# First-layer modulation products in steps of 256 columns instead of 512

## The chip, the cores and the metric

The kernel runs on one core of one Trainium2 chip. The metric is the device time of one execution in microseconds (us), the median of several runs. A second number is used beside it: one execution was taken by the hardware profiler, and all views of the trace come from that one.

## The reference

Two layers of a trunk for a diffusion model. Each layer has a mixer and an MLP, and around both of them an adaptive norm (shift, scale, gate). The six modulation vectors of a layer come from one product, of a vector per condition with a weight of 1024 x 6144:

```python
def _modulation(cond, w, b):
    m = jax.nn.silu(cond) @ w + b
    return jnp.split(m[:, None, :], 6, axis=-1)
...
    p_sh1, p_sc1, p_g1, p_sh2, p_sc2, p_g2 = _modulation(c_ctx[None, :], ada_w[l], ada_b[l])
    s_sh1, s_sc1, s_g1, s_sh2, s_sc2, s_g2 = _modulation(c, ada_w[l], ada_b[l])
    hp = _rmsnorm(xp, norm_g[l, 0]) * (1.0 + p_sc1) + p_sh1
    hs = _rmsnorm(xs, norm_g[l, 0]) * (1.0 + s_sc1) + s_sh1
    ...
    xp = xp + p_g1 * mp
    xs = xs + s_g1 * ms
    hp = _rmsnorm(xp, norm_g[l, 1]) * (1.0 + p_sc2) + p_sh2
    hs = _rmsnorm(xs, norm_g[l, 1]) * (1.0 + s_sc2) + s_sh2
    xp = xp + p_g2 * _mlp(hp, w_mlp1[l], w_mlp2[l])
    xs = xs + s_g2 * _mlp(hs, w_mlp1[l], w_mlp2[l])
```

There are 128 context tokens (`xp`) and 256 latent ones (`xs`), of width 1024, all in float32. The mixer of layer 0 is a pair of recurrences, HGRN2 and a gated delta rule; the delta rule solves triangular systems of 32 x 32. The mixer of layer 1 is neighbourhood attention.

## The kernel before, in words

Tokens are held as three tiles of 128, the width 1024 as eight k-tiles of 128 (`KT`). Weights are loaded as float32, split into a high part (`whi`, L209) and a low part (`wlo`, L210), and each product is three matmuls: high by high, low by high, high by low (rows L646 to L648 and L688 to L690 of the profile, 384 or 256 columns each).

Layer 0 (`layer0`) writes its work in an order set by hand, the string `STEPS` (L55 to 58). Each word is a piece: `f`, `q`, `c`, `v`, `g` are blocks of projections of the tokens, `h` a step of the HGRN2 recurrence, `d` a step of the delta rule, `a` a step of the modulation products, and a number behind `h`, `d` or `a` is a count of such steps. The framework's scheduler then places the instructions of each engine by its own simulation, so the order on an engine isn't the order of the string word for word.

The modulation products of layer 0 come in three parts. The shift and scale for the mixer are made in front of all else (L446, in passes of 256 columns). The change is in the other two, which `ada_rest` (L373) makes while the mixer runs:

- `ada_quad` (L314): the columns 2048 to 4095 (gate of the mixer and shift of the MLP), as 4 groups of 512 columns. It takes 8 steps, one for each k-tile. A step loads two tiles of 512 KB (L324) and runs 4 matmuls (L327); each has a stationary of 32 columns (the conditions) and a moving operand of 512 columns, and writes 32 of the 128 rows of one accumulator (`ada`). Four such matmuls use four column groups of the PE array.
- `ada_half` (L354): the columns 4096 to 5119 (scale of the MLP) as 2 groups of 512 columns, with the 8 k-tiles as two halves in parallel: 4 steps, each again with two tiles of 512 KB (L363) and 4 matmuls (L368).

The tiles come from a ring of two (`adr=2` in the pool `spa`). A step takes both, so its loads wait until the matmuls of the step before are done with them. Behind `ada_quad` the gate goes to memory (`gs`, L389) and the shift is spread over partitions (L489).

SP issues all loads and stores of the kernel in one order, and a load that waits for its ring holds back what stands behind it: the weight loads (`raw`, L204), the ring's loads (`adr`), and the way in and out of the triangular solve: `g` to memory and back (`s`, `sm`: L1057, L1058, L1062), the solve on GpSimd (L1071, L1072 in turn, 31 times), its result to memory (`s<-sm`, L1074) and back (`hyB<-s`, L1076). TensorE's L1105 and DVE's L1078 wait for hyB. The convolution of the delta rule has a pair of operations on GpSimd (L947, L948) between the solve's; TensorE's transpose (L953) waits for it.

## Time and profile before

| what | value |
|---|---|
| median of 3 runs | 1148.52 us (1146.92 to 1149.19) |
| the profiled execution, its own time | 1152.35 us |
| its span in the trace | 1150.6 us |
| mean granted TensorE clock | 0.976 |
| TensorE busy | 1088.7 us (95%), 6861 instructions |
| DVE, ACT, POOL busy | 760.7, 490.1, 289.9 us |
| L327 matmuls | 71.6 to 175.8 us |
| L368 matmuls | 198.9 to 281.3 us |

Times in rows are microseconds from the start of the span. A row of the chain of waits has a start, a length and what ran; a row of the timeline has the same with the engine, line, tiles and shapes, and in brackets the idle time ahead of it with what ended it. `SPq` is the queue of SP, which issues transfers. One float32 matmul of the program shows as two records, so four matmuls are "x8".

### The profile page before, as it was taken

To read this page: it belongs to the slowest core of one execution; us is meant where nothing else is said; L and a number is where in the kernel's file an instruction comes from. 1 tells how busy PE (TensorE), PEld (TensorE's weight loads), DVE (VectorE), ACT (ScalarE), POOL (GpSimd) and SP (SyncE) were. 2 spreads that over 40 slices of the span, in tenths; PEclk is the share of its full clock that TensorE was granted. 3 is DMA by queue.
4 is the path that set the end of the run, shared out by engine and by line. 5 is a ranking of instruction groups with operands and counts; after the bars stand their busy time and mean duration, and the time that the engine had idled before them with its cause. 6 is when DMAs were issued, how large, how long until landed. Compare 5 with 4: busy or idle time off the path is not lost.

```text
span 1150.6 us, 18007 instructions
## 1 busy us (share of the span) xinstructions
PE 1088.7 (95%) x6861; PEld 943.6 (82%) x6861; DVE 760.7 (66%) x1186; ACT 490.1 (43%) x874; POOL 289.9 (25%) x301
## 2 busy tenths in 40 slices
PE   6989978999899899999999989999988999999998
PEld 3868767988888888898889878888768889989987
DVE  3678598895356697986898565877757763333333
ACT  3465333333354553333343455555635433433330
POOL 0064894231222210120121334424012011101102
PEclk9989988999799899999999999999999999999999
DMA  8953624333043597775774228666524964333311
GB/s 283 292 166 112 215 97 131 114 109 126 19 129 110 176 318 274 255 245 178 238 242 161 74 55 196 192 181 158 142 74 126 331 192 138 128 114 125 110 37 56
DMA packets 142091, 184.66 MB, mean 160 GB/s; under 512 B 36803, under 2 KB 113685, under 8 KB 142005
## 3 DMA queue, kind: packets, MB, share of 16 engines
q1 hardware_dynamic: 141685, 183.44, 50.6%
q8 instruction: 54, 0.88, 0.3%
q14 instruction: 32, 0.26, 0.1%
q10 hardware_dynamic: 320, 0.07, 0.0%
HBM read 171.53 MB, written 4.61 MB: 153 GB/s over the span
## 4 chain that ended last, share of the span: by engine, by line
PE 73%; DMA 7%; POOL 7%; DVE 6%; SPq 3%; issue 2%; ACT 2%; POOLq 0%; DVEq 0%; ACTq 0%
PE acc L1344 7%; PE tmp L1359 7%; PE tmp L1360 7%; PE acc L1346 7%; PE acc L1345 7%; PE tmp L1358 7%; POOL sm L1071 2%; POOL sm L1072 2%; DMA ada<-in_ada_w 2%; PE acc L646 2%; PE acc L647 2%; PE po L1735 2%; PE acc L673 2%; PE acc L674 1%; PE acc L648 1%
## 5 line engine op out<-in xcount | busy, mean ns | idle before, releaser
L209 ACT ACTIVATE whi<-raw 128x1024 fp32r<-128x1024 f32 x198 | 205.9, 1050 | 331.3 <-PE acc L1346 212.0
L210 DVE TENSOR_TENSOR wlo<-raw,whi 128x1024 fp32r<-128x1024 f32 x192 | 237.3, 1246 | 162.7 <-ACT whi L209 159.4
L1378 POOL TENSOR_TENSOR h<-h 128x384 f32<-128x384 f32 x56 | 69.9, 1248 | 423.7 <-ACT h L1375 408.2
L1345 PE MATMUL acc<-wlo,h 128*128 128x512 f32 x380 | 148.5, 391 | 0.0
L1344 PE MATMUL acc<-whi,h 128*128 128x512 f32 x380 | 146.2, 393 | 0.1
L347 DVE SCALAR_TENSOR_TENSOR adc<-adr,scz,adc 128x1024 f32<-128x1024 f32 x98 | 127.8, 1335 | 9.4 <-DMA adr<-in_ada_w 9.2
L1346 PE MATMUL acc<-whi,h 128*128 128x512 f32 x380 | 121.1, 391 | 0.0
L1344 PEld LDWEIGHTS acc<-whi,h 128*128 128x128 f32 x380 | 71.1, 188 | 20.1 <-ACT whi L209 5.6
L1359 PE MATMUL tmp<-hyA,whi 128*128 128x384 f32 (+1 forms) x256 | 85.2, 333 | 2.1 <-DVE hyA L566 2.1
L1358 PE MATMUL tmp<-hyA,whi 128*128 128x384 f32 (+1 forms) x256 | 84.3, 335 | 1.5 <-ACT whi L209 1.5
L1360 PE MATMUL tmp<-hyA,wlo 128*128 128x384 f32 (+1 forms) x256 | 84.9, 333 | 0.0
L1358 PE MATMUL tmp<-hyB,whi 128*128 128x384 f32 (+1 forms) x256 | 83.7, 329 | 1.2 <-DVE hyB L565 1.2
L1359 PE MATMUL tmp<-hyB,whi 128*128 128x384 f32 (+1 forms) x256 | 84.1, 329 | 0.7 <-DVE hyB L566 0.7
L1345 PEld LDWEIGHTS acc<-wlo,h 128*128 128x128 f32 x380 | 71.4, 188 | 14.0 <-DVE wlo L210 0.2
L1346 PEld LDWEIGHTS acc<-whi,h 128*128 128x128 f32 x380 | 71.0, 188 | 13.7
L1360 PE MATMUL tmp<-hyB,wlo 128*128 128x384 f32 (+1 forms) x256 | 82.1, 328 | 0.0
L646 PE MATMUL acc<-hyA,whi 128*128 128x384 f32 x208 | 74.7, 359 | 0.9 <-DVE hyB L707 0.9
L647 PE MATMUL acc<-hyA,whi 128*128 128x384 f32 x208 | 72.3, 348 | 0.0
L648 PE MATMUL acc<-hyA,wlo 128*128 128x384 f32 x208 | 72.0, 347 | 0.0
L1379 DVE TENSOR_TENSOR h<-h,h 128x384 fp32r<-128x384 f32 (+2 forms) x72 | 38.5, 535 | 41.1 <-POOL h L1378 40.5
L526 POOL TENSOR_TENSOR ss<-ss,eps 128x1 f32<-128x1 f32 (+2 forms) x30 | 35.7, 1194 | 68.9 <-DVE ss L545 21.1
L1359 PEld LDWEIGHTS tmp<-hyA,whi 128*128 128x128 f32 x256 | 49.3, 193 | 3.3 <-DVE hyA L566 2.3
(458 smaller groups left out, 2402.9 us busy)
## 6 DMA issues: line engine op xcount, KB each, us to landing
raw<-in_w_mlp SPq DMA_DIRECT2D x128, 512.0 KB, 3.8
adr<-in_ada_w SPq DMA_DIRECT2D x80, 512.0 KB, 4.7
raw<-in_w_in_ab SPq DMA_DIRECT2D x34, 512.0 KB, 4.5
ada<-in_ada_w SPq DMA_DIRECT2D x32, 256.0 KB, 5.5
raw<-in_w_qkv_na SPq DMA_DIRECT2D x32, 256.0 KB, 3.1
raw<-in_w_out_ab SPq DMA_DIRECT2D x8, 512.0 KB, 4.0
m<-gs SPq DMA_DIRECT2D x8, 512.0 KB
raw<-in_w_qkv_na SPq DMA_DIRECT2D x8, 512.0 KB
```

Source lines behind the costliest of these rows:

```text
L209: self.nc.scalar.activation(hi, x, AF.Copy)
L210: (eng or self.nc.vector).tensor_tensor(lo, x, hi.bitcast(F32), op=ALU.subtract)
L347: nc.vector.scalar_tensor_tensor(acc[v], raw, s[v], acc[v], op0=ALU.mult, op1=ALU.add)
L646: nc.tensor.matmul(pg[n], whi(k)[:, c], hhi[:, k], start=(k == 0), stop=False)
L647: nc.tensor.matmul(pg[n], whi(k)[:, c], hlo[:, k], start=False, stop=False)
L648: nc.tensor.matmul(pg[n], wlo(k)[:, c], hhi[:, k], start=False, stop=(k == KT - 1))
L1344: nc.tensor.matmul(pg, shi, w2hi(n)[:, o], start=start, stop=False)
L1345: nc.tensor.matmul(pg, shi, w2lo(n)[:, o], start=False, stop=False)
L1346: nc.tensor.matmul(pg, slo, w2hi(n)[:, o], start=False, stop=last)
L1358: nc.tensor.matmul(pg[n], w1hi(k)[:, c], hhi[:, k, tc_], start=(k == 0), stop=False)
L1359: nc.tensor.matmul(pg[n], w1hi(k)[:, c], hlo[:, k, tc_], start=False, stop=False)
L1360: nc.tensor.matmul(pg[n], w1lo(k)[:, c], hhi[:, k, tc_], start=False, stop=(k == KT - 1))
```

## The change

The modulation products go in half steps. The outer loop is now over the two halves of 256 columns of each group of 512, and the inner over the k-tiles. A half step takes one tile of the ring, 512 KB, and runs its 4 matmuls on 256 columns. In `ada_quad` one transfer fills a tile, with runs of 1 KB where it had 4 KB before; in `ada_half` there are two transfers of 256 KB for each tile. `ada_rest` has 24 steps where it had 12, and the counts behind `a` in `STEPS` are doubled in the same places. The ring stays at two tiles, and all bytes are the same.

```diff
-d f3 f1 f2 d q1 a2 q0 d h a2 h a h c4 h a d h3 d c5 h a2 d h v0 h d h d v1 a d h3
-c0 h3 c1 h5 d2 h d2 h d h7 g0 g1 d m g2 g3 a3
+d f3 f1 f2 d q1 a4 q0 d h a4 h a2 h c4 h a2 d h3 d c5 h a4 d h v0 h d h d v1 a2 d h3
+c0 h3 c1 h5 d2 h d2 h d h7 g0 g1 d m g2 g3 a6
...
-        for kt in range(KT):
-            w = []
-            for j in range(0, 4, 2):
-                raw = self.sb([P, 2, 512], self.ada_ring)
-                rows = i["ada_w"][l, kt * P:(kt + 1) * P]
-                nc.sync.dma_start(raw, rows[:, cols[j]:cols[j] + D].rearrange("p (j n) -> p j n", j=2))
-                w += [raw[:, n] for n in range(2)]
-            for j in range(4):
-                nc.tensor.matmul(pm[32 * j:32 * j + 32], self.sc[:, 2 * kt:2 * kt + 32], w[j], start=(kt == 0), stop=(kt == KT - 1))
-            if kt < KT - 1:
-                yield
+        for c in range(2):
+            for kt in range(KT):
+                w = self.sb([P, 4, 256], self.ada_ring)
+                rows = i["ada_w"][l, kt * P:(kt + 1) * P, col:col + 4 * 512]
+                nc.sync.dma_start(w, rows.rearrange("p (j c n) -> p j c n", j=4, c=2)[:, :, c])
+                for j in range(4):
+                    nc.tensor.matmul(pm[32 * j:32 * j + 32, 256 * c:256 * c + 256], self.sc[:, 2 * kt:2 * kt + 32], w[:, j],
+                                     start=(kt == 0), stop=(kt == KT - 1))
+                if c == 0 or kt < KT - 1:
+                    yield
...
-        for r in range(4):
-            w = []
-            for g in range(2):
-                w.append(self.sb([P, 2, 512], self.ada_ring))
-                nc.sync.dma_start(w[g], i["ada_w"][l, (4 * g + r) * P:(4 * g + r + 1) * P, col:col + D].rearrange("p (n c) -> p n c", n=2))
-            for g in range(2):
-                kt = 4 * g + r
-                for n in range(2):
-                    j = 2 * g + n
-                    nc.tensor.matmul(pm[32 * j:32 * j + 32], self.sc[:, 2 * kt:2 * kt + 32], w[g][:, n], start=(r == 0), stop=(r == 3))
-            if r < 3:
-                yield
+        for c in range(2):
+            for r in range(4):
+                w = self.sb([P, 2, 2, 256], self.ada_ring)
+                for g in range(2):
+                    rows = i["ada_w"][l, (4 * g + r) * P:(4 * g + r + 1) * P, col:col + D]
+                    nc.sync.dma_start(w[:, g], rows.rearrange("p (n c m) -> p n c m", n=2, c=2)[:, :, c])
+                for g in range(2):
+                    kt = 4 * g + r
+                    for n in range(2):
+                        j = 2 * g + n
+                        nc.tensor.matmul(pm[32 * j:32 * j + 32, 256 * c:256 * c + 256], self.sc[:, 2 * kt:2 * kt + 32], w[:, g, n],
+                                         start=(r == 0), stop=(r == 3))
+                if c == 0 or r < 3:
+                    yield
```

In the new file every line from `ada_rest` on has a number higher by 2 (L1105 is L1107, L688 is L690); L327 becomes L326, L363 and L368 become L364 and L369.

The scheduler moves instructions around these steps. Three places matter to the prediction. The first is on PE, where it comes to the first matmul on the solve's result (`gd<-hyB`); `acc` are product rows, `hyA` the normed tokens. Before:

```order
L688 MATMUL acc_2209<-whi_2201,hyA_128 128x256
L689 MATMUL acc_2209<-whi_2201,hyA_129 128x256
L690 MATMUL acc_2209<-wlo_2202,hyA_128 128x256
L1105 MATMUL gd_927<-hyB_649,m_120_753 32x32 [waits DMAHW4_49]
L1105 MATMUL gd_927<-hyB_649,m_120_753 32x32 x11
L1105 MATMUL gd_940<-hyB_649,m_120_753 32x32 x12
L953 MATMUL tmp_1876<-ident,cv_1873 128x128 [waits Pool_49] x2
L953 MATMUL tmp_1876<-ident,cv_1873 128x128
L688 MATMUL acc_2209<-whi_2205,hyA_130 128x256
```

Now:

```order
L690 MATMUL acc_2241<-whi_2237,hyA_130 128x256
L691 MATMUL acc_2241<-whi_2237,hyA_131 128x256
L692 MATMUL acc_2241<-wlo_2238,hyA_130 128x256
L1107 MATMUL gd_927<-hyB_649,m_120_753 32x32 [waits DMAHW3_49]
L1107 MATMUL gd_927<-hyB_649,m_120_753 32x32 x11
L1107 MATMUL gd_940<-hyB_649,m_120_753 32x32 x12
L690 MATMUL acc_2241<-whi_2233,hyA_128 128x256
L691 MATMUL acc_2241<-whi_2233,hyA_129 128x256
L692 MATMUL acc_2241<-wlo_2234,hyA_128 128x256
```

Before, 36 rows of this `acc` stand ahead of the wait for hyB and 12 behind it; now 24 stand ahead and 24 behind. The transpose L953 (now L955) moves further back.

The second place is on SP, around the store of the solve's result (`s<-sm`) and its way back (`hyB<-s`). Before:

```order
L204 DMA raw_2542<-in_w_in_ab 128x4x256 [waits DMAHW6_49,DVE_49]
L363 DMA adr_2287<-in_ada_w 128x1024 [waits DMAHW1_49,PE_49]
L1074 DMA s_842<-sm_139_850 24x32x32 [waits Pool_49]
L1074 DMA s_842<-sm_139_850 24x32x32
L1074 DMA s_842<-sm_139_850 24x32x32 [waits DMAHW7_49]
L1074 DMA s_842<-sm_139_850 24x32x32 [waits DMAHW0_49]
L363 DMA adr_2289<-in_ada_w 128x1024 [waits DMAHW2_49,PE_49]
L389 DMA gs_1940<-ada_1260 2x512 [waits DVE_49]
L389 DMA gs_1940<-ada_1260 2x512 [waits DMAHW3_49]
L1076 DMA hyB_649<-s_842 128x768 [waits DMAHW6_49,DMAHW5_49,DMAHW7_49,DMAHW4_49,DMAHW0_49]
```

Now:

```order
L204 DMA raw_2580<-in_w_in_ab 128x4x256 [waits DMAHW6_49,DVE_49]
L1076 DMA s_842<-sm_139_850 24x32x32 [waits Pool_49]
L1076 DMA s_842<-sm_139_850 24x32x32 x2
L1076 DMA s_842<-sm_139_850 24x32x32 [waits DMAHW7_49]
L364 DMA adr_2319<-in_ada_w 128x2x256 [waits DMAHW1_49,DMAHW0_49,PE_49]
L364 DMA adr_2319<-in_ada_w 128x2x256
L364 DMA adr_2326<-in_ada_w 128x2x256 [waits DMAHW2_49,PE_49]
L1078 DMA hyB_649<-s_842 128x768 [waits DMAHW6_49,DMAHW5_49,DMAHW7_49,DMAHW4_49,DMAHW3_49]
L391 DMA gs_1972<-ada_1260 2x512 [waits DVE_49]
L391 DMA gs_1972<-ada_1260 2x512
L364 DMA adr_2326<-in_ada_w 128x2x256
```

The load that stood ahead of the stores now stands behind them, so three loads of 256 KB go out between the stores and hyB where one of 512 KB did; the two gate stores and a fourth load come behind hyB.

The third place is on PE again, later, where the second and third steps of `ada_half` stood. Before (`hg` and `gd` are the recurrences' matmuls):

```order
L368 MATMUL ada_2286<-adr_3349,scz 32x512 [waits DMAHW7_49]
L368 MATMUL ada_2286<-adr_3349,scz 32x512
L368 MATMUL ada_2286<-adr_3351,scz 32x512 [waits DMAHW0_49]
L368 MATMUL ada_2286<-adr_3351,scz 32x512
L832 MATMUL hg_2909<-ident,x 128x128 [waits DVE_49]
...
L368 MATMUL ada_2286<-adr_3357,scz 32x512 [waits DMAHW2_49]
L368 MATMUL ada_2286<-adr_3357,scz 32x512
L832 MATMUL hg_2938<-ident,x 128x128 [waits Activation_49]
L832 MATMUL hg_2938<-ident,x 128x128 x3
L368 MATMUL ada_2286<-adr_3359,scz 32x512 [waits DMAHW3_49]
L368 MATMUL ada_2286<-adr_3359,scz 32x512
```

Now, from the second tile of this stretch on:

```order
L369 MATMUL ada_2318<-adr_3394,scz 32x256 [waits DMAHW4_49]
L765 MATMUL hg_2910<-hq_1451,km_2908 128x128 [waits DVE_49,Activation_49]
...
L369 MATMUL ada_2318<-adr_3394,scz 32x256
L834 MATMUL hg_2947<-ident,x 128x128 [waits DVE_49]
...
L369 MATMUL ada_2318<-adr_3408,scz 32x256 [waits DMAHW0_49]
L369 MATMUL ada_2318<-adr_3408,scz 32x256
L839 MATMUL hg_2954<-hyB_650,km_2952 128x128 [waits DVE_49,Activation_49]
...
L369 MATMUL ada_2318<-adr_3408,scz 32x256 [waits DMAHW1_49]
L369 MATMUL ada_2318<-adr_3408,scz 32x256
```

Matmuls of the recurrences now stand between the matmuls of one step. Over all of `ada_half` there are nine groups with other rows between them, where there were five. On GpSimd, the pair L947, L948 that L953 waits for stands three iterations of the solve earlier than before, and the next such pair stands behind the solve.

More of the change, by code (lines that the diff above doesn't have):

```diff
@@ L311, in params, with ada_quad @@
         nc.vector.tensor_scalar(self.lb1, self.lb, -1.0, 1.0, op0=ALU.mult, op1=ALU.add)
-    def ada_quad(self, l, cols, take):
+    def ada_quad(self, l, col, take):
         nc, i = self.nc, self.i
         pm = self.ps([P, 512], "ada")
-        for kt in range(KT):
-            w = []
-            for j in range(0, 4, 2):
-                raw = self.sb([P, 2, 512], self.ada_ring)
-                rows = i["ada_w"][l, kt * P:(kt + 1) * P]
-                nc.sync.dma_start(raw, rows[:, cols[j]:cols[j] + D].rearrange("p (j n) -> p j n", j=2))
-                w += [raw[:, n] for n in range(2)]
-            for j in range(4):
-                nc.tensor.matmul(pm[32 * j:32 * j + 32], self.sc[:, 2 * kt:2 * kt + 32], w[j], start=(kt == 0), stop=(kt == KT - 1))
-            if kt < KT - 1:
-                yield
+        for c in range(2):
[8 more added lines that the diff above has]
+                    yield
         take(slice(0, P), pm)
@@ L385, in take @@
             nc.vector.tensor_copy(rows[64:], pm[64:])
-        yield from self.ada_quad(0, [2 * D, 2 * D + 512, 3 * D, 3 * D + 512], take)
+        yield from self.ada_quad(0, 2 * D, take)
         scr = self.gate[0, 0] = self.dp.tile([2, D], F32, tag="gs00", name="gs00")
```

## The prediction

> **What bounds the kernel now.** First the page's head: what the engines are busy with, and what makes up the chain that ended last.
>
> ```profile
> PE 1088.7 (95%) x6861; PEld 943.6 (82%) x6861; DVE 760.7 (66%) x1186; ACT 490.1 (43%) x874; POOL 289.9 (25%) x301
> PE 73%; DMA 7%; POOL 7%; DVE 6%; SPq 3%; issue 2%; ACT 2%; POOLq 0%; DVEq 0%; ACTq 0%
> ```
>
> TensorE is 73% of the chain. The other 27% are stages in which something else ends last, and the modulation products that change (L327, L368) lie in and around such a stage. So the second view is the windows over the larger part of their stretch, cut where the bound changes. The columns are window, length, busy time of PE, PEld, DVE, ACT and POOL with counts, granted clock, DMA share and GB/s.
>
> ```profile
> 110.00:182.00 72.00, 59.04 (x580) 48.66 (x573) 56.02 (x62) 25.03 (x39) 60.58 (x75) 0.90 0.47 151
> ...
> 192.50:293.00 100.50, 98.31 (x1108) 89.04 (x1108) 80.48 (x150) 35.10 (x61) 23.24 (x30) 0.97 0.33 104
> ```
>
> PE works 59.04 of 72 us in the first window, where GpSimd works 60.58, and 98.31 of 100.50 in the second: it idles before 182, and is full from 192.5 on. The third view, the chain of waits in order of time, says why (start, length, what):
>
> ```profile
> 81.37 1.65 PE hg L991 x6
> 83.66 1.85 PE ada L327 x4
> 85.52 1.30 PE hg L991 x6
> ...
> 107.82 4.84 DMA s<-g
> 114.36 3.63 DMA sm<-s
> 118.19 0.55 POOL sm L1071
> ...
> 183.49 3.17 DMA s<-sm
> 186.68 5.83 DMA hyB<-s
> 192.56 1.60 PE gd L1105 x48
> ...
> 198.94 0.99 PE ada L368 x8
> ...
> 254.64 1.02 PE ada L368 x8
> 255.67 4.54 DMA adr<-in_ada_w
> ...
> 260.25 1.05 PE ada L368 x4
> ...
> 261.88 0.98 PE ada L368 x4
> ...
> 280.26 1.00 PE ada L368 x8
> ```
>
> From 107.8 to 192.5 the chain is the solve on GpSimd (L1071, L1072) with its way in and out of memory. So of the eight quad steps only one piece is on the chain, the 1.85 us of L327 at 83.66; the other L327 matmuls lie under the solve. Behind 192.5 all of L368 is on it: 0.99 + 1.02 + 1.05 + 0.98 + 1.00 = 5.04 us, and one wait for a weight tile.
>
> **The change part by part.** The bytes are the same, and so is the count of 512 KB tiles. The ring stays at two, so the step that runs after two prefetched halves still loads on demand: by the number of tiles in flight nothing is won. What remains is how the pieces fall.
>
> *Front, 71 to 110 us.* In the new order no modulation matmul stands between the two L991 groups. What caps the gain is the time for which the Activation engine, next on the chain, sat idle until PE was done:
>
> ```profile
> 87.07 0.28 ACT L958 ACTIVATE cv<-tmp 128x128 f32<-128x128 f32 x1 [0.79 <-PE tmp L953]
> ```
>
> I take −0.8 us. The ends are 0 (something else is late next) and −1.85 (the whole piece goes).
>
> *Under the solve, 110 to 182 us.* The L327 pieces get shorter or move; GpSimd has no gap there, and its time covers them: 0. Uncovered they would cost as a whole step does, about 1 us each.
>
> *The hyB load.* SP issues in order. Before, one 512 KB load (adr) goes out between the solve's stores and hyB, the other ahead of the stores; now three loads of 256 KB go out there.
>
> ```profile
> 184.51 0.75 SPq L363 DMA_DIRECT2D adr<-in_ada_w  x1
> 186.68 0.34 SPq L1076 DMA_DIRECT2D hyB<-s  x1
> ```
>
> The window around it (columns as above):
>
> ```profile
> 186.00:188.00 2.00, 2.00 (x74) 1.96 (x74) 1.97 (x5) 2.00 (x4) 0.00 (x0) 1.00 0.99 257
> ```
>
> The transfers are full there (0.99, 257 GB/s), so 256 KB more ahead of hyB is 1.0 us later if it shares nothing, 0 if it is done by 186.7. I take +0.5 (0 to +1.7, the whole second tile plus the issue times).
>
> *What PE has left when hyB comes.* hyB is waited for by the L1105 row, and PE takes its rows in order: all that stands behind L1105 waits too. Before, 36 product rows (L688 to L690) stand between the last L758 and L1105; now 24. The 12 that move behind it cost what one advances, 0.12 us (190.82 − 190.70):
>
> ```profile
> 190.70 0.28 PE L688 MATMUL acc<-whi,hyA 128*128 128x256 f32 x1
> 190.82 0.28 PE L689 MATMUL acc<-whi,hyA 128*128 128x256 f32 x1
> ...
> 192.56 0.62 PE L1105 MATMUL gd<-hyB,m 32*32 32x32 f32 x14 [1.33 <-DMA hyB<-s]
> ```
>
> Where they stood they ran in time that nobody missed; behind the wait, where PE is full, they cost 12 x 0.12 = +1.4 us (0 if PE is so late that hyB isn't waited for). PE's idle time ahead of hyB grows from 1.33 to about 1.33 + 1.4 + 0.5 = 3.3 us. It grows further: the convolution pair L947/L948 that PE waits for before 180.2 is done three solve iterations earlier on GpSimd in the new order, and these lie between 177.65 and 179.70.
>
> ```profile
> 177.65 0.33 POOL L1071 TENSOR_TENSOR sm<-sm,sm 96x87 f32<-96x87 f32 x1
> 179.70 0.45 POOL L947 TENSOR_TENSOR cv<-cv,cv 128x128 f32<-128x128 f32 x1
> 180.20 0.47 PE L953 MATMUL tmp<-ident,cv 128*128 128x128 f32 x1 [3.02 <-POOL cv L947]
> ```
>
> So PE's work is up to 2.1 us earlier, and its gap ahead of hyB 3.3 to 5.4 us long.
>
> *The clock after that gap.* The granted clock falls to half after a stretch in which PE did little:
>
> ```profile
> 158.08:161.48 3.40, 0.21 (x2) 0.21 (x3) 3.40 (x4) 0.28 (x1) 3.24 (x5) 1.00 0.00 0
> 161.49:164.90 3.41, 3.41 (x39) 2.98 (x42) 3.41 (x5) 0.83 (x3) 3.25 (x4) 0.50 0.02 5
> ...
> 188.80:192.20 3.40, 2.42 (x21) 2.22 (x19) 1.94 (x4) 0.00 (x0) 1.70 (x2) 1.00 0.89 257
> ...
> 192.20:195.61 3.41, 3.05 (x61) 3.02 (x62) 3.03 (x5) 0.49 (x1) 2.00 (x4) 1.00 0.38 134
> ```
>
> 0.21 us of work in a 3.4 us stretch was followed by a granted clock of 0.50 (the second row); after 2.42 us (the stretch ahead of hyB) PE stayed at full clock, 1.00 in the last row. With a gap of 3.3 to 5.4 us that stretch holds at most about 1 us of work, and the next 3.41 us, all on the path now, run at half clock: half of it is lost, +1.7 us (0 to +3.4, if a second stretch follows).
> [...]
>
> *L368 becomes nine groups.* Before, five groups of 512 columns, 5.04 us. In the new order the eight half steps' 32 matmuls come as nine groups with other matmuls between: four of five to seven matmuls, two steps' worth of time, and five of one or two. A full group of 256 columns costs what the products at the front of the kernel show, where eight passes of four matmuls run together:
>
> ```profile
> 42.53 1.86 PE ada L446 x32
> ```
>
> That is 1.86 / 4 = 0.465 us for a step of 256 columns; alone I add what a 512 group has over twice that, 1.00 − 0.93 = 0.07: 0.53. A group of one or two col groups lasts as long as one of four. 5 x 0.53 + 4 x 1.0 = 6.6 us, +1.6 against 5.04. The ends are 8 x 0.465 = 3.7 (−1.3, all steps whole and contiguous) and 13 pieces x 0.6 = 7.8 (+2.8).
> [...]
>
> *The wait in r2.* PE waits 1.68 us for a weight tile:
>
> ```profile
> 260.25 1.05 PE L368 MATMUL ada<-adr,scz 128*32 128x512 f32 x4 [1.68 <-DMA adr<-in_ada_w]
> ```
>
> and SP's queue waits for the ring (total, times, longest):
>
> ```profile
> SPq L363 <- PE ada L368: 18.1, 4, 10.9
> ```
>
> SP stands 18.1 us waiting for the ring in L363, so loads go out the moment a tile is free. A half step frees its tile after half the matmuls, so the next load leaves earlier by about half of a group; I take half the wait away, −0.8 (−1.68 if it goes, +1.0 if a second such wait appears at the sixth step).
>
> The sum is −0.8 + 0.5 + 1.4 + 1.7 + 1.6 − 0.8 = +3.6 us. The profiled execution took 1152.35 us (0.33% over the median of the runs, 1148.52), so it would give 1155.95; on the median that is 1152.1. About 0.2%, 2.3 us, is what a measurement can tell from no change.
>
> **The rivals.**
> *No half clock, one window (chance 0.30, within 0.2%).* The edges of the stretches fall so that neither holds an idle one, or PE is later than I think. For it: 1.72 us of work around the 1.68 us gap at 258.57 was followed by full clock.
>
> ```profile
> 257.06:260.46 3.40, 1.72 (x15) 1.41 (x16) 3.40 (x10) 1.09 (x3) 0.00 (x0) 1.00 0.88 307
> 260.47:263.87 3.40, 3.40 (x22) 1.64 (x19) 1.65 (x4) 1.16 (x4) 1.51 (x2) 1.00 0.76 246
> ```
>
> The sum is then +1.9, 1150.4. That the change doesn't do what it says, since two tiles still leave the last half of a step on demand, ends here too (1148.5).
> *Faster (0.20).* The place is L368 behind 192.5: if the four matmuls of a step stand together and their tile has landed when PE comes to them, the groups cost 3.7 (−1.3) and the wait at 260 goes (−1.68); with −1.85 at the front, hyB no later and the 12 rows (+1.4), that is −3.4, 1145.1. It decides by whether loads of 1 KB runs land within the time between two groups. Against it: the order has the groups cut apart, and the medians of issue to landing are alike, 4.7 for adr and 4.5 for raw of 1 KB runs (both 512 KB):
>
> ```profile
> adr<-in_ada_w SPq DMA_DIRECT2D x80, 512.0 KB, 4.7
> raw<-in_w_in_ab SPq DMA_DIRECT2D x34, 512.0 KB, 4.5
> ```
>
> *Two stretches at half clock (0.10).* The gd groups behind hyB are small, and the second stretch counts as idle too: +5.3, 1153.8.
>
> **How the numbers follow.** The forecast has 0.40, and with the last rival slower has 0.50; the first rival is the 0.30 within 0.2% (1146.2 to 1150.8), faster 0.20. The range begins at 1145.8, below which half of the faster case lies, and ends at 1154.5, which takes in most of two stretches at half clock.
>
> **What would show each step.** In the changed kernel: L991 groups with nothing between (front); the issue of hyB to its landing longer than 5.83 us; a wait for hyB of 3 us or more with PEclk near 0.5 in the 3.4 us behind it; 24 L690 rows behind L1107; L369 groups that sum to 6 to 7 us on the chain; one wait for adr of less than 1.7 us around 260. The prediction is wrong if the wait for hyB stays under 2 us, if the clock behind it stays full, or if L369 sums to less than 5 us.

## The result and the profile after

The kernel after takes 1159.58 us (median of 4 runs, 1157.03 to 1164.07) where the kernel before takes 1148.48 (4 runs, 1146.92 to 1149.19): slower by 11.1 us, ratio 1.0103 [1.007, 1.0136]. The forecast was slower by 3.6, and its range ended 5.1 us short. The profiled execution after took 1159.7 us, with a span of 1157.6. One run of before, among those taken beside the `spread` kernels, took 1778.28 us at a granted clock of 0.555, and the ratios leave it out.

The page of after, the rows that answer to the two of before: busy time of the engines, and what makes up the chain that ended last.

```profile
PE 1088.6 (94%) x6957; PEld 947.3 (82%) x6957; DVE 764.3 (66%) x1186; ACT 489.5 (42%) x874; POOL 279.0 (24%) x301
PE 77%; DVE 6%; POOL 6%; DMA 5%; ACT 2%; issue 2%; SPq 2%; ACTq 0%; POOLq 0%; DVEq 0%
```

TensorE is as busy as before (1088.6 against 1088.7 us) with 96 more matmul records, and it is now 77% of the chain where it was 73%: the loss is on PE's side and not in the solve. Over the fixed window of the solve PE's work is less and its clock lower in this execution (0.86 against 0.90; columns: window, length, busy PE, PEld, DVE, ACT, POOL, granted clock, DMA share, GB/s):

```profile
110.00:182.00 72.00, 54.56 (x585) 46.55 (x584) 53.03 (x61) 23.35 (x36) 58.98 (x72) 0.86 0.47 140
```

Since the two kernels do the same things at other times, fixed windows don't compare stages; markers do. I cut the traces at the first modulation matmul on `adr`, the solve's first and last instruction, the first matmul on hyB, the first matmul on `ones` of the key products (L1024, L1026 in after), and the first layer's MLP. Both kernels were profiled twice. Lengths in us, each pair the two executions:

```
stage                                    before            after            mean
first ada<-adr to solve's start          46.55  46.19      46.68  46.60     +0.3
solve                                    63.61  63.38      63.25  63.86     +0.1
solve's end to first gd<-hyB             10.75  10.00      10.00  11.26     +0.3
first gd<-hyB to first gd<-ones          96.40  96.43     103.67 104.63     +7.7
from there to the first layer's MLP     109.74 108.76     109.47 109.88     +0.4
the first layer's MLP                   264.16 264.12     264.52 264.50     +0.4
from its end to the second layer's MLP  228.00 228.84     230.92 231.12     +2.6
rest                                    259.72 259.14     259.15 259.21     -0.3
```

That sums to +11.5, against 11.1 of the medians. The table begins at a marker some 70 us into the kernel; the stretch ahead of it, which holds no matmul of the changed steps, took 71.64 and 71.14 us before and 69.93 and 70.81 after, 1.0 less in the mean, so the whole spans differ by 10.5. Two thirds lie in the one stage behind hyB, which holds all of L368 (L369). Its rows, before (first and second execution) and after (first and second):

```profile
192.56:288.95 96.39, 94.26 (x1082) 85.47 (x1083) 77.44 (x143) 34.58 (x60) 23.24 (x30) 0.98 0.34 108
```

```profile
190.71:287.14 96.43, 94.26 (x1082) 85.49 (x1083) 77.54 (x143) 34.58 (x60) 23.26 (x30) 0.98 0.36 110
```

```profile
189.86:293.53 103.67, 100.08 (x1127) 90.73 (x1127) 80.00 (x148) 34.46 (x60) 22.60 (x32) 0.97 0.35 107
```

```profile
192.53:297.16 104.63, 101.15 (x1126) 92.06 (x1127) 80.17 (x148) 34.45 (x60) 22.57 (x32) 0.95 0.35 105
```

PE has 44 or 45 matmul records more (32 from the halved columns, 12 product rows), is busy 5.8 and 6.9 us longer, and idles 3.6 and 3.5 us instead of 2.1 and 2.2. The mean clock of the stage falls from 0.98 to 0.97 and 0.95.

The chain of waits of after, in order of time (start, length, what):

```profile
79.69 1.65 PE hg L993 x6
81.55 1.64 PE hg L993 x8
...
181.56 4.35 DMA s<-sm
185.99 3.82 DMA hyB<-s
189.86 1.60 PE gd L1107 x48
...
199.22 0.55 PE ada L369 x2
...
252.54 0.99 PE ada L369 x14
...
255.51 0.55 PE ada L369 x2
...
257.54 1.01 PE ada L369 x8
258.57 5.52 DMA adr<-in_ada_w
264.14 0.63 PE ada L369 x4
...
293.53 4.25 PE gd L1026 x24
```

At the front no modulation matmul stands between the L993 groups any more, as forecast, and they are through in 3.9 us (79.69 to 83.63) where they took 5.5 (81.37 to 86.82). In these rows x2 is one matmul, 0.55 us, and x14 is seven, 0.99 us, which is what the forecast set for such pieces. The x8 at 257.54 is four of a group of six that came apart into three pieces of two; with the wait inside it the group ends at 260.0. In place of one wait for a tile there are two, and a third wait, for another engine, has grown. After, by the timeline (in brackets the idle time ahead and its releaser), then before:

```profile
259.39 0.63 PE L369 MATMUL ada<-adr,scz 128*32 128x256 f32 x4 [0.86 <-DMA adr<-in_ada_w]
...
264.14 0.63 PE L369 MATMUL ada<-adr,scz 128*32 128x256 f32 x4 [0.95 <-DMA adr<-in_ada_w]
...
293.53 4.25 PE L1026 MATMUL gd<-ones,g 128*128 128x1 f32 x24 [1.77 <-DVE m L1016]
```

```profile
288.95 3.22 PE L1024 MATMUL gd<-ones,g 128*128 128x1 f32 x24 [0.46 <-DVE m L1014]
```

The third thing in this stage is the clock. The stretches around hyB in after:

```profile
188.79:192.20 3.41, 2.79 (x58) 2.55 (x58) 3.22 (x7) 0.00 (x0) 2.14 (x4) 1.00 0.91 289
192.20:195.61 3.41, 3.41 (x19) 3.41 (x17) 3.24 (x8) 0.00 (x0) 1.01 (x2) 0.50 0.30 102
```

Behind hyB (189.86) one stretch of 3.41 us ran at half clock with PE full: 1.7 us lost. In the second execution it was two stretches, 3.4 us. Such a stretch is no mark of the new kernel alone. In the second execution of before one stands in the same place (hyB at 190.71), in a stage of 96.43 us:

```profile
189.68:193.09 3.41, 2.38 (x55) 2.34 (x56) 2.37 (x4) 0.26 (x1) 2.00 (x4) 1.00 0.68 223
193.09:196.50 3.41, 3.41 (x18) 3.41 (x17) 3.27 (x8) 0.83 (x2) 0.00 (x0) 0.50 0.00 0
```

What differs is their number in the stage: one in both executions of before, two and three in those of after.

### The profile page after: what moved, and what is told of

Same layout as the page of the kernel before. It is cut to its first block, busy times and chain, and to the rows that moved or that the text cites. A ratio compares the mean times of both kernels' runs of the same rounds, so it can differ in the third digit from the quotient of the medians.

```text
span 1157.6 us, 18223 instructions
## 1 busy us (share of the span) xinstructions
PE 1088.6 (94%) x6957; PEld 947.3 (82%) x6957; DVE 764.3 (66%) x1186; ACT 489.5 (42%) x874; POOL 279.0 (24%) x301
## 4 chain that ended last, share of the span: by engine, by line
PE 77%; DVE 6%; POOL 6%; DMA 5%; ACT 2%; issue 2%; SPq 2%; ACTq 0%; POOLq 0%; DVEq 0%
PE tmp L1361 8%; PE tmp L1362 7%; PE tmp L1360 7%; PE acc L1346 7%; PE acc L1347 7%; PE acc L1348 7%; POOL sm L1074 2%; POOL sm L1073 2%; PE acc L648 2%; PE acc L649 2%; PE acc L650 2%; PE acc L675 2%; PE acc L676 2%; PE po L1737 1%; PE acc L677 1%
## 5 line engine op out<-in xcount | busy, mean ns | idle before, releaser
L210 DVE TENSOR_TENSOR wlo<-raw,whi 128x1024 fp32r<-128x1024 f32 x192 | 240.7, 1264 | 164.6 <-ACT whi L209 155.9
L1380 POOL TENSOR_TENSOR h<-h 128x384 f32<-128x384 f32 x56 | 65.8, 1175 | 427.8 <-ACT h L1377 413.3
L1360 PEld LDWEIGHTS tmp<-hyA,whi 128*128 128x128 f32 x256 | 48.7, 192 | 4.4 <-ACT km L563 3.4
L1361 PEld LDWEIGHTS tmp<-hyA,whi 128*128 128x128 f32 x256 | 49.1, 192 | 3.2 <-DVE hyA L568 2.3
```

Source lines behind the costliest of these rows:

```text
L210: (eng or self.nc.vector).tensor_tensor(lo, x, hi.bitcast(F32), op=ALU.subtract)
L1360: nc.tensor.matmul(pg[n], w1hi(k)[:, c], hhi[:, k, tc_], start=(k == 0), stop=False)
L1361: nc.tensor.matmul(pg[n], w1hi(k)[:, c], hlo[:, k, tc_], start=False, stop=False)
```

## The experiments

**The theories.** The first: the loss is the forecast's own terms at another size, and lies in L369's groups, the rows behind hyB and the clock. Its rivals: the loads, now smaller and placed otherwise in SP's queue, bring it; or the 256-column matmuls themselves do, by the order that follows from them; or it is one wait that the new order adds.

**1. Each part alone.** `quad_only` has the new `ada_quad` with the old `ada_half`; `half_only` the reverse. Beside those functions, `STEPS` of the first and of the second:

```diff
-d f3 f1 f2 d q1 a2 q0 d h a2 h a h c4 h a d h3 d c5 h a2 d h v0 h d h d v1 a d h3
+d f3 f1 f2 d q1 a4 q0 d h a4 h a2 h c4 h a2 d h3 d c5 h a4 d h v0 h d h d v1 a d h3
...
-d f3 f1 f2 d q1 a2 q0 d h a2 h a h c4 h a d h3 d c5 h a2 d h v0 h d h d v1 a d h3
-c0 h3 c1 h5 d2 h d2 h d h7 g0 g1 d m g2 g3 a3
+d f3 f1 f2 d q1 a2 q0 d h a2 h a h c4 h a d h3 d c5 h a2 d h v0 h d h d v1 a2 d h3
+c0 h3 c1 h5 d2 h d2 h d h7 g0 g1 d m g2 g3 a6
```

> Half steps in the quad part alone; the half part keeps its steps of 512 columns. In the order 6 product rows instead of 12 move behind the wait for hyB (0.7 us), and behind it stand seven groups of L368 instead of five (about +2 us). Theory of the order (the loss is TensorE work that leaves the solve's shadow, and groups cut apart): +2.5 to +4 us against before. Rival, loads (1 KB runs and loads that leave one tile at a time cost by themselves): two thirds of the bytes are in this part, so about 7 of the 11 us. Rival, clock (stretches at half clock fall otherwise): any of -3 to +5, and the stage from hyB to L1024 within 1 us of 96.4 once its stretches at half clock are taken out.

> Half steps in the half part alone. In the order 7 product rows move behind the wait for hyB (0.8 us); L369 comes as eight groups of which two hold six or seven matmuls, about 5.2 us by 0.53 and 1.0 a group against 4.84 (+0.4). Theory of the order: +1 to +3 us. Rival, loads: a third of the bytes, about 4 us, with waits for adr behind 250 us that are longer than the 1.68 us of before. Rival, clock: as above.

Measured: `quad_only` 1156.88 against 1149.09, +7.8, ratio 1.0068 [1.0047, 1.0089]; `half_only` 1152.81, +3.7, ratio 1.0035 [1.0019, 1.0051]. The two sum to 11.5, so within the intervals the parts add. The larger one is the quad steps, whose own matmuls the forecast had as a gain at the front and as nothing under the solve. The next runs take each part apart.

**2. The width without the loads.** `narrow_mm` keeps the steps and loads of before and splits each matmul into two of 256 columns; `quad_narrow`, run later, does so in `ada_quad` alone.

```diff
-            for j in range(4):
-                nc.tensor.matmul(pm[32 * j:32 * j + 32], ..., w[j], start=(kt == 0), stop=(kt == KT - 1))
+            for c in range(0, 512, 256):
+                for j in range(4):
+                    nc.tensor.matmul(pm[32 * j:32 * j + 32, c:c + 256], ..., w[j][:, c:c + 256],
+                                     start=(kt == 0 and c == 0), stop=(kt == KT - 1 and c == 256))
```

> Steps and loads as before (two tiles of 512 KB, runs of 4 KB), but each step runs its matmuls as twice four of 256 columns. In the order all 36 product rows stay ahead of the wait for hyB. Theory of the order: no rows displaced, groups of 8, 6, 2, 1, 7, 2, 6 matmuls cost 5.6 to 6.5 us against 4.84, so +0.5 to +2 us. [...] Rival, loads: 0.

> Loads and steps as before; the quad part's step runs its matmuls as twice four of 256 columns, the half part is unchanged. By the order 36 product rows ahead of hyB as before and L368 in groups of 4, 4, 2, 2, 2, 2. Work alone: L368 about 5.3 instead of 4.84, +0.5. Theory that shorter quad matmuls bring the loss (narrow_mm lost 8.8 with the loads of before): +5 to +8. Rival (the loads of half steps, one tile at a time, bring it): within 1.5 us of before.

Measured: `narrow_mm` 1157.89, +8.8, ratio 1.0079 [1.0049, 1.011]; `quad_narrow` 1157.23 against 1149.90, +7.3, ratio 1.0066 [1.0045, 1.0087]. With all loads as before, the narrow quad matmuls alone cost as much as the whole quad part. So the loss of that part comes without its loads. The runs of `quad_narrow` one by one go with the clock: the two at a mean granted clock of 0.978, as before, took 1151.57 and 1152.08 us, the two at 0.971 took 1160.51 and 1160.15. Over the 11 runs one microsecond lost to the clock is one microsecond of time (slope 1.01, 87% of the variance); in the runs of before the slope is 0.49 (45%), in those of `half_only` 0.20 (6%). Its trace shows one place where clock is lost (the stretch before hyB and the two behind):

```profile
188.46:191.87 3.41, 0.79 (x7) 0.59 (x5) 2.32 (x5) 0.00 (x0) 1.24 (x1) 0.98 0.98 317
191.87:195.30 3.43, 3.17 (x52) 3.10 (x52) 3.12 (x6) 0.00 (x0) 2.01 (x4) 0.50 0.74 250
195.30:198.70 3.40, 3.40 (x19) 3.40 (x18) 3.31 (x7) 1.05 (x2) 0.00 (x0) 0.52 0.00 0
```

PE had 0.79 us of work in the stretch before hyB and then ran two stretches at half clock (0.50 and 0.52), as the forecast had it behind a stretch with little work, here without any of the change's loads. But this trace is of the fastest run, 1151.57 us, and its stage behind hyB is 98.44 us long, 2.0 more than before. Where most of its other runs lose 5 to 10 us more, no trace shows.

**3. The loads without the pieces.** `half_oneload` is `half_only` with one transfer of 512 KB for a tile (4 KB runs) in place of two of 256 KB (1 KB runs); it reads other weights than the reference wants, in the same amount. `after_oneload` is the same edit on after.

```diff
-                for g in range(2):
-                    rows = i["ada_w"][l, (4 * g + r) * P:(4 * g + r + 1) * P, col:col + D]
-                    nc.sync.dma_start(w[:, g], rows.rearrange("p (n c m) -> p n c m", n=2, c=2)[:, :, c])
+                k = 2 * r + c
+                nc.sync.dma_start(w.rearrange("p g n m -> p (g n m)"), i["ada_w"][l, k * P:(k + 1) * P, col:col + D])
```

> Half steps in the half part alone, as in half_only, but each tile is filled by one load of 512 KB with runs of 4 KB instead of two of 256 KB with runs of 1 KB; the weights so loaded are the wrong ones, so the scale of the MLP is not the reference's. By the order 36 product rows stay ahead of hyB (half_only: 29) and the L369 matmuls come in groups of 8, 8, 4, 4, 4, 3, 1 (half_only: 4, 4, 1, 7, 6, 2, 4, 4). Theory of the pieces: two loads a tile, each with its own landing to wait for, are what cuts the steps apart; about 4.6 us in L369, no rows displaced, 0 to +1.5 us against before, 2.5 to 4 better than half_only. Rival (half steps of 256 columns cost by themselves): as half_only, +4.

> The changed kernel with the same edit (one load of 4 KB runs for each tile of the half part, wrong weights and so a wrong scale of the MLP). By the order six groups of 2, 6, 8, 4, 4, 8 matmuls behind hyB where the changed kernel has nine, and 30 product rows ahead of it instead of 24. Theory of the pieces: L369 about 5 us instead of 7, rows 0.7 us less, so 3 to 5 us better than the changed kernel: +6 to +8 against before. Rival (width): +10 to +12.

Measured: `half_oneload` 1149.66 against 1149.82, ratio 1.0 [0.9984, 1.0015]; `after_oneload` 1158.72, +8.9, ratio 1.0069 [1.0048, 1.009]. The half part's loss is gone whole. The matmuls of this line alone, in the stage behind hyB (window, busy PE, then PEld, clock, DMA), in before, `half_only`, `half_oneload` and after:

```profile
192.56:288.95 96.39, 5.30 (x32) 0.76 (x32) 0.98 0.34 108
```

```profile
190.95:290.69 99.74, 6.74 (x64) 1.75 (x64) 0.97 0.35 106
```

```profile
192.22:289.10 96.88, 5.31 (x64) 1.60 (x64) 0.98 0.35 107
```

```profile
189.86:293.53 103.67, 7.97 (x64) 2.32 (x64) 0.97 0.35 107
```

The 32 matmuls of 256 columns (64 records) cost 5.31 us where 16 of 512 (32 records) cost 5.30, if a step's four have one load to wait for; with two, the matmuls of one step come apart and the same 64 records cost 6.74 and 7.97. So for the half part it was the loads of a tile, not the width. The edit changes two things, the number of loads and the length of their runs, and no run takes these apart. That PE waits longer for data isn't it: it idles 2.1 us in this stage in `half_only` and in before. What differs there is the order on PE, with groups cut and seven product rows behind hyB, and two stretches at half clock in the stage instead of one. In after, the same edit gives back 2.2 us of 11.1, with intervals that overlap; most of the loss stays.

**4. The groups of L368 whole, with the new quad steps.** `quad_whole` is `quad_only` with one step of the old `ada_half` moved in `STEPS` to where the groups of L368 fall whole.

```diff
-d f3 f1 f2 d q1 a4 q0 d h a4 h a2 h c4 h a2 d h3 d c5 h a4 d h v0 h d h d v1 a d h3
-c0 h3 c1 h5 d2 h d2 h d h7 g0 g1 d m g2 g3 a3
+d f3 f1 f2 d q1 a4 q0 d h a4 h a2 h c4 h a2 d h3 d c5 h a4 d h v0 h d h d v1 d h3
+c0 a h3 c1 h5 d2 h d2 h d h7 g0 g1 d m g2 g3 a3
```

> Half steps in the quad part alone, as in quad_only, but the one step called behind v1 is called three words later. By the order that changes one thing behind hyB: the L368 matmuls come as five groups of 4, 4, 2, 2, 4, as in the kernel before, where quad_only had seven of 2, 2, 2, 2, 2, 2, 4; still 30 product rows ahead of hyB. Theory of the pieces: L368 falls from 6.3 to about 4.8 us, and with it some of the stretches at half clock; 2 to 4 us better than quad_only, so +4 to +6 against before. Rival (the half steps under the solve cost it, by the rows that move or by the clock): as quad_only, +7 to +8. Rival (chance: stretches at half clock fall otherwise in every build): anything from +2 to +9 with the same 4.8 us.

Measured: 1156.36 against 1149.82, +6.5, ratio 1.0062 [1.0038, 1.0086]. The row of L368 reads as in before, and the stage is still 4.4 us longer than before's, in an execution that took 1161.01 us, 4.7 over the median:

```profile
191.22:292.03 100.81, 5.30 (x32) 0.76 (x32) 0.95 0.35 106
```

By the medians the cut groups of L368 explain about 1.3 of the quad part's 7.8 us, which the intervals can't tell from nothing. The mean clock in this stage is 0.95, against 0.98.

**5. The rows that moved.** `rows_behind` is before with the twelve product rows L688 to L690 of one block held back until hyB; `conv_late` is before with the three transposes L953 held back instead; `rows_conv` does both. (In the order on PE after, both stand behind.)

```diff
+                with self.tc.issue_after(self.mark["hyB"].ins) if t in late else ExitStack():
                     for k in range(KT):
                         nc.tensor.matmul(pg[:, t - t0], hhi[:, k, c], whi(k), ...)
...
+            with self.tc.issue_after(self.mark["hyB", 1].ins) if n == 10 else ExitStack():
                 for t in range(NT):
                     nc.tensor.transpose(pt[:, t], dst[:, t], self.c["ident"])
```

> The kernel before, with the product rows of the last two token tiles of v1 held behind the first L1105 matmuls: by the order 12 rows fewer of the products stand ahead of hyB, as in the changed kernel, and one step of L368 (4 of the 16 matmuls) moves ahead of it; no half steps anywhere. The work alone: 12 rows x 0.12 = +1.4, one step of L368 less behind hyB -1.0, so +0.4 us. Theory that the displaced rows also bring the stretches at half clock (the kernels with 480 to 486 product rows ahead of hyB lost 3.4 to 5.1 us to them between hyB and L1024, those with 492 mostly 1.7): +2 to +4 us, with half clock right behind hyB. Rival (half steps bring them, by another way): within 1 us of before and 1.7 us lost to half clock in that stage.

> The kernel before, with the three transposes (L953) of one convolution, which stand right behind the first L1105 group, held behind the second: all else of TensorE's order stays. In the orders of the changed kernel, quad_only, quad_whole and half_only these transposes also come some 24 product rows later. Theory that this is what the slow builds share: +2 to +4 us, with a second stretch at half clock between hyB and L1024. Rival (it is of no account): within 1 us.

> rows_behind and conv_late together, no half steps: the order of the changed kernel around hyB without its modulation steps. If the order around hyB brings the stretches at half clock: +2 to +5 us. If they come with the half steps themselves: within 1 us of before, as rows_behind.

Measured: `rows_behind` 1150.89 against 1150.55, ratio 1.0012 [0.9996, 1.0027]; `conv_late` 1154.72 against 1149.90, +4.8, ratio 1.0042 [1.0025, 1.0059]; `rows_conv` 1149.94, ratio 1.0004 [0.9991, 1.0016]. In `rows_behind` one step of L368 went the other way, ahead of hyB (24 records of 32 are left behind it), and its stage is 96.53 us long: twelve rows at +1.4 less a step of 1.0 would be +0.4, and +0.3 was measured. The rows bring no further half clock:

```profile
192.10:288.63 96.53, 94.75 (x1077) 86.55 (x1077) 77.92 (x143) 34.35 (x60) 23.11 (x30) 0.98 0.36 110
```

`conv_late` is a warning. Three transposes moved cost 4.8 us, and with the twelve rows moved too it costs nothing. Two waits of PE are in its trace that before has smaller or not at all:

```profile
PE gd L1025 <- DVE A L491: 2.2, 1, 2.2
PE ada L368 <- DMA adr<-in_ada_w: 2.1, 1, 2.1
```

So a few instructions' place in this stage moves the time by as much as either part of the change, and no rule that I have says which way.

**6. The wait before the key products.** In after and in the builds with narrow quad matmuls (not in `quad_only`) PE waits 1.7 to 1.8 us ahead of L1024 (L1026), for a vector chain that starts at the four small matmuls of L489. The `spread` kernels order those four behind the products of L1012, on before, on after and on `quad_narrow`.

```diff
+            with ExitStack() as st:
+                for t in range(NT if late else 0):
+                    st.enter_context(self.tc.issue_after(self.mark["attn", t].ins))
                 nc.tensor.matmul(pt[:, q], rows[:, q * P:(q + 1) * P], pick, start=True, stop=True)
```

> The kernel before with the same edit: there the wait was 0.5 us and two of the eight records of the spread filled it already. All theories: within 1.5 us of before; a gain of more than 1.5 us would be a version that beats both.

> The changed kernel, with the four spread matmuls of the scale (L491) held behind the last L1014 matmuls, so that they fill the time for which TensorE waited for DVE there (1.8 us in both traces). Nothing else of TensorE's order changes. Theory that this wait is a main part of the loss: 1.3 us of waiting less and with it half clock, so 3 to 5 us better than the changed kernel, +6 to +8 against before. If only the wait itself counts: 1 to 1.5 us better, +9.5 to +10. If it is of no account (DVE's chain is as late): +10.5 to +11.5.

> quad_narrow with the same edit. Theory of the wait: +2 to +4 against before instead of +7.3. Wait alone: about +6. No account: +7.

Measured: before 1149.77 against 1149.55, ratio 1.0 [0.9983, 1.0016]; after 1160.56, ratio 1.0093 [1.0067, 1.0119]; `narrow_spread` 1156.37, ratio 1.0051 [1.003, 1.0073]. Nothing is won back beyond the noise. In the spread build of after PE's wait there is 1.0 us and the stage 102.6 instead of 103.7, but the time is that of after; the stretch between the two MLPs is 233.6 us long in its trace instead of 230.9. Taking that wait away doesn't shorten the kernel.

**7. How the clock and the work behind hyB price other edits of before.** `early` does four modulation steps ahead of where they stood; `half_twice` runs each L368 matmul twice, which doubles that product; `scalar_way` issues the solve's stores and its load back on the Activation queue.

```diff
-d f3 f1 f2 d q1 a2 q0 d h a2 h a h c4 h a d h3 d c5 h a2 d h v0 h d h d v1 a d h3
-c0 h3 c1 h5 d2 h d2 h d h7 g0 g1 d m g2 g3 a3
+d f3 f1 f2 d q1 a2 q0 d h a2 h a2 h c4 h a2 d h3 d c5 h a4 d h v0 h d h d v1 d h3
+c0 h3 c1 h5 d2 h d2 h d h7 g0 g1 d m g2 g3
...
+                    for again in range(2):
+                        nc.tensor.matmul(..., start=(r == 0 and again == 0), stop=(r == 3 and again == 1))
...
-            nc.sync.dma_start(sy(s2, b), X[24 * b:24 * b + 24])
+            nc.scalar.dma_start(sy(s2, b), X[24 * b:24 * b + 24])
...
-        nc.sync.dma_start(f(XC), s2.rearrange("p d c -> p (d c)"))
+        nc.scalar.dma_start(f(XC), s2.rearrange("p d c -> p (d c)"))
```

> The kernel before with its modulation steps called earlier in the list (all but the last done before the value blocks): in the order 44 of the 48 L327 and L368 matmuls stand ahead of hyB instead of 36 of 48 counted in calls of four columns groups, but 18 more product rows stand behind it. Theory of the order: L368 behind hyB falls from 4.84 to about 2 us and its wait of 1.68 goes, 18 rows cost 2.2 us: -2 to -3 us, unless hyB comes later. Rival, loads: more loads ahead of the solve's way back hold hyB up, +1 to +3 us. Rival, clock: within 2 us of before.

> The kernel before, with each L368 matmul run twice into the same rows (so the scale of the MLP comes out doubled): nothing else of the order ahead of hyB changes, 36 product rows stay there, and behind hyB stand 32 matmuls of 512 columns in groups of 8, 6, 2, 8, 2, 5, 1 instead of 16. Work theory: TensorE's work behind hyB counts one for one: +4.8 to +6 us. Rival, slack (other engines have hidden some of L368 all along): +2 us or less. [...]

> The kernel before, with the solve's way out and back (s<-sm and hyB<-s) issued by the Activation engine instead of SP, so that it isn't queued behind the loads of weights and adr. Theory that hyB's landing sets the time of all behind it: it comes 1 to 4 us earlier, and 44 product rows stand ahead of it instead of 36; -1 to -4 us. Rival (the transfers share the same engines, whoever issues them): within 1 us; and if Activation's own work waits behind the issue, +1 to +3 us.

Measured: `early` 1152.94 against 1149.09, +3.9, ratio 1.0037 [1.0021, 1.0053]; `half_twice` 1154.91 against 1149.87, +5.0, ratio 1.0033 [1.0015, 1.0052]; `scalar_way` 1153.73, +3.9, ratio 1.0029 [1.0009, 1.005]. In `early` 24 of the 32 L368 records left the stage, and it got longer (98.03). PE comes to its first matmul on hyB 13.1 us after the solve's end instead of 10.8, and without a wait: product rows and a wait of 1.5 us for a weight tile stand ahead of it now. Two stretches at half clock stand 21 us behind it. In `half_twice` L368 does 12.52 us of work instead of 5.30, and PE's idle time in the stage, 2.1 us, is gone: 5 of 7 us arrive by the medians. In `scalar_way` hyB lands 9.2 us after the solve's end, where it took 10.7 and 10.0 in the two executions of before, but PE comes to it only at 10.7, without a wait. In its profiled execution, which took 1161.76 us, 8 over the median, 17 us of half clock appear 20 us behind it:

```profile
211.50:228.80 17.30, 17.02 (x193) 15.79 (x194) 11.29 (x21) 2.78 (x5) 6.62 (x9) 0.51 0.20 61
```

**8. Second executions.** One more profile each of before and after, for the pairs of the table above.

> The kernel before once more, for a second trace. Work theory (groups cut apart, rows behind hyB): the stage from hyB to the matmuls of L1024 is 96.4 us within one stretch at half clock (1.7 us) again, and its idle and half-clock parts add to about 4 us. Chance theory (stretches at half clock fall where they will, and the first trace was a lucky one): the stage comes out at 98 us or more, and the attention of layer 1 holds a stretch at half clock as in the changed kernel.

> The changed kernel once more, for a second trace. Work theory: the stage from hyB to the same point is 103.7 us within 1.7 us, with 7 us of L369 and 48 product rows of 256 columns in it, and half clock right behind hyB again. Chance theory: the stage without its idle and half-clock parts stays at about 96.7, but these parts fall to about 4 us, so that the stage is 100 to 101 us.

They took 1149.79 and 1164.02 us. In after PE waited 4.54 us for hyB in this execution, 0.62 in the first; the stage's length moved by 1.0.

**The clock over all runs.** The time lost to the clock is (1 − mean granted clock) x time. Over 128 runs of before it is 25.6 us (mean clock 0.9778, mean time 1149.9); one more, at a clock of 0.929, took 1152.25 us and is left out. Differences from that, by the means of the runs:

```
kernel          time    lost to the clock   the rest
after          +10.2          +5.2            +5.0
quad_only       +7.4          +3.4            +4.0
quad_whole      +6.3          +4.5            +1.8
quad_narrow     +7.4          +5.1            +2.3
narrow_mm       +8.7          +4.6            +4.1
after_oneload   +7.9          +6.3            +1.6
after_spread   +11.1          +5.2            +5.9
narrow_spread   +6.7          +6.5            +0.2
half_only       +3.6          +3.4            +0.2
conv_late       +4.9          +4.4            +0.5
early           +3.3          +4.1            -0.9
half_twice      +4.7          +2.9            +1.8
scalar_way      +4.7          +7.0            -2.3
rows_behind     +1.6          +0.5            +1.1
rows_conv       +0.5          +0.6            -0.2
half_oneload     0.0          -0.2            +0.1
before_spread   +0.1          +0.2            -0.1
```

Every build that is more than 1.6 us slower loses 2.9 us or more to the clock, `half_twice` too, which got nothing but more work. Part of that loss lies under the solve, whose length it didn't move (in after 63.25 us at a mean clock of 0.85 in the first execution, 63.86 at 0.92 in the second), so the column is an upper bound; the run at 0.929 lost 56 us more by this account and was 2.4 us slower. It is a companion of the loss, not by itself its cause. No kernel tried beats before.

## Why the prediction was right and wrong

The sign was right, the size was not: 3.6 us forecast, 11.1 measured. The wait in r2 failed outright, the gap ahead of hyB came in one execution of the two, and the term that it put at nothing, the quad steps under the solve, is where most of the loss comes from. Term by term, from the two executions of each kernel; in the stage behind hyB, +7.7 us are +2.1 groups, +1.5 rows, +2.6 clock, +1.4 idle time and +0.2 that I can't place.

- *Front, −0.8 forecast, +0.3 measured.* The matmuls moved as said and the L993 groups were through 1.5 us sooner, but the chain behind them took it back. Four of its links, after and then before:

```profile
103.83 3.21 DVE L1054 TENSOR_TENSOR hyB<-hyB,cd 128x384 f32<-128x384 f32 x2
104.22 2.41 POOL L210 TENSOR_TENSOR wlo<-raw,whi 128x1024 fp32r<-128x1024 f32 x1 [9.81 <-ACT whi L209]
```

```profile
105.71 1.01 DVE L1052 TENSOR_TENSOR hyB<-hyB,cd 128x384 f32<-128x384 f32 x2
107.89 2.40 POOL L210 TENSOR_TENSOR wlo<-raw,whi 128x1024 fp32r<-128x1024 f32 x1 [11.13 <-ACT whi L209]
```

GpSimd's L210, which came behind this pair of multiplies before, now runs beside it, and one of the two takes 2.7 us instead of 0.55. It is so in all nine traces with narrow quad matmuls (2.2 to 2.8 us) and in none of the other eleven. The store behind it (`s<-g`) then landed in 2.47 us instead of 4.84, so what this costs in the end no run shows.

- *Under the solve, 0 forecast, +0.1 measured.* The solve takes 63.2 to 63.9 us in both, so GpSimd's time does cover PE's there, as forecast. What the term left out is what the quad steps do elsewhere: alone they cost 6.5 to 7.8 us in three builds, one of them with no load changed.
- *hyB, +0.5 forecast, +0.3 measured,* inside the spread of two executions (10.0 to 11.3). SP issued the load back later (6.1 and 6.6 us after the solve's end instead of 4.9 and 5.1), since the last store of the solve's result took 4.35 us to land in after's chain and 3.17 in before's; the load itself took 3.82 us instead of 5.83. So the three loads ahead of it did not lengthen it; whether they lengthened the store's landing no run shows.
- *The gap ahead of hyB,* 3.3 to 5.4 us forecast, was 0.62 us in the first execution and 4.54 in the second. In the first, then, the sign that the forecast gave for being wrong (under 2 us) came true: with twelve rows fewer PE was through with what stands ahead of hyB 9.4 us after the solve's end, as in the first execution of before.
- *Rows behind hyB, +1.4 forecast, +1.5 measured.* `rows_behind` fits the price, but its interval is too wide to confirm it.
- *L369 in groups, +1.6 forecast, +2.1 measured:* L368 took 4.84 us and L369 7.04 and 6.76, where the time in which a matmul's end lies beside its neighbour is counted once (the rows above, 5.30 and 7.97, count it twice). The nine groups came as forecast, and what exceeds the price is the one of six matmuls: set at 1.0, it came as three pieces and took 1.6 and 1.3 without its wait. `half_oneload`, with one load for a tile, has 5.31 in that row. (The forecast's "eight passes" of L446 are four, 16 matmuls in 32 records; its division by four is right.)
- *The clock, +1.7 forecast, +2.6 measured.* The stage loses 3.41 and 5.12 us to half clock where it lost 1.71 in both executions of before. In after one stretch right behind hyB is there, as forecast, and two in the second execution; the rival "two stretches at half clock" was the truth in one execution of the two. Over all traces half clock stands within 3 us of hyB in nine of the ten with narrow quad matmuls or with two loads for a tile of L369 (not in `quad_only`, where it comes 20 us later), and in one of the ten others, the second execution of before. The forecast's reason was the long gap ahead of hyB. In the first execution the stretch came behind a gap of 0.62 us, so there the term came out by luck; the second, with 4.54 us, fits the reason. The rows and transposes that move are not enough to bring it: `rows_conv` moves them in before, has a gap of 1.03 us and loses nothing.

  The forecast had half clock behind a stretch with little work. `quad_narrow`'s row agrees in kind (0.79 us of work in 3.41, then 0.50). In after 2.79 us of work and in the second execution of before 2.38, in both partly the 32x32 matmuls on hyB (1.6 us in all), were followed by 0.50 too, where 2.42 us in the first execution of before were followed by 1.00. So busy time by the trace doesn't tell when the clock falls.
- *The wait in r2, −0.8 forecast.* This step failed outright. It was one wait of 1.68 us for a weight tile; it became two, 0.86 and 0.95 (0.65 and 1.06 in the second execution), as in the forecast's end "if a second such wait appears", and nothing was won. My reading, not tested by itself: a tile is free sooner, but the next step needs two landings. A wait that the forecast has no term for grew with it: 1.77 in place of 0.46 ahead of L1026, for DVE. With both, PE's idle time in the stage rose by 1.4.
- *What had no term.* Behind L1026 the forecast took the rest of the kernel as unchanged. The stretch from the first layer's MLP to the second's is 2.6 us longer, though the order of instructions on every engine is the same there. In the nine traces with narrow quad matmuls it takes 231.1 us in the mean (228.8 to 233.6), in the eleven without 228.6 (226.1 to 230.9). This stays open; PE's waits in that stretch (for `ks`, for `v` of L1682) differ as much between two executions of one kernel as between kernels.

By the traces 7.9 us are missing (11.5 less 3.6). Gains that didn't come and waits that grew instead are 3.3 of them (front 1.1, PE's idle time 2.2), terms that were too small 1.5 (clock 0.9, groups 0.5, rows 0.1), and 3.1 had no term at all (2.6 in the second layer, 0.4 and 0.4 on the way there, less 0.3 at the end).

What stays open: why 256-column matmuls in `ada_quad`, with the same bytes, loads and steps, cost 7 us. In the three traces with the old loads PE waits 2.9 to 3.1 us for hyB, in the builds of before with the old quad steps 0 to 1.5; in the traces with the new quad loads it is anything from 0.6 to 4.5. PE's idle time under the solve is 13.8 to 18.1 us in the nine traces with narrow quad matmuls and 12.2 to 13.5 in those with the old quad steps (16.0 in `half_oneload`, which loses nothing), so idle time there is not enough as a reason. The width and the order that the scheduler makes of it were not taken apart.

## What to carry to other kernels

Halving the work of a step won nothing here. With one load for a tile the half part cost nothing (`half_oneload`); with two it cost 3.7 us, since a step's four matmuls came apart, and a piece costs as much as or more than a whole one: 0.55 us for one matmul and 0.63 for two in after, where four of L446 that stand together took 0.47 in before (1.86 for 16). The quad part had one load for a tile and lost 7 us all the same, so work that lies under another engine's time is not free to change: look at what the new order does to the stages around it, and build that part alone. And in a kernel whose order a scheduler decides, test an edit's parts one at a time, and beside them edits that only move instructions (here `conv_late` and `rows_conv`): moves of three instructions were worth 4.8 us or nothing.

## What the hardware showed

- Four matmuls of 256 columns on four column groups cost the same as half of a 512-column step when the four stand together (64 records for 5.31 us in `half_oneload` against 32 for 5.30 in before). One such matmul alone took 0.55 us in after, and seven 0.99.
- In the first execution of after the granted clock fell to 0.50 for a stretch of 3.41 us behind one in which PE was busy for 2.79 us by the trace, partly with 32x32 matmuls, and in the second execution of before behind 2.38 us; in the first execution of before it stayed at 1.00 behind 2.42 us (188.80 to 192.20).
- One of a pair of equal VectorE multiplies (128x384) took 2.75 us in after, where a GpSimd subtraction of 2.41 us ran beside it, and the other 0.55; in before, where none did, both took 0.55.
- Runs of one and the same kernel, `quad_narrow`, spread over 9.7 us (1151.57 to 1161.3) with the mean granted clock, 0.978 to 0.971.
